# A two-layer encoder trunk on one core: first weights in halves, turns block by block, Silu behind the last norm, and the last norm's second column half prepared ahead

## The chip, the core and the metric

The kernel runs on one core of one Trainium2 chip. The metric is the device time of one execution in microseconds. TensorE is PE in the profile (its weight loads are PEld), VectorE is DVE, ScalarE is ACT, GpSimd is POOL, SyncE is SP; SPq, ACTq and POOLq are the queues from which these engines issue DMAs.

## The reference: what is computed

Two requests, 512 and 256 tokens of 1024 features, go through the same two layers. Each layer is a macaron block, and a final RMSNorm closes the trunk:

```python
x = x + 0.5 * swiglu_ffn(rmsnorm(x, g0), w1a, w2a)    # D 1024, DFF 2816
x = x + mixer(rmsnorm(x, g1))                          # layer 0: HGRN2, layer 1: windowed attention
x = x + 0.5 * swiglu_ffn(rmsnorm(x, g2), w1b, w2b)

def swiglu_ffn(x, w1, w2):
    gate, up = split(x @ w1)
    return (silu(gate) * up) @ w2
```

All is float32. The first operation is thus RMSNorm of the input and the first half of a feed-forward (called f0 in the kernel), the last is a feed-forward's second product, the residual add, and RMSNorm with the gain `g_final`.

## The kernel before

The 768 tokens are six blocks of 128 rows, three to a half (`H` = 384 tokens). A float32 product is made of three products in the format f32r: a tile is split into a high part (a CAST on ACT) and a low part (a subtraction on DVE), and `mm3` (L368 to L370) adds high by high, high by low and low by high. Most of the feed-forwards' products go by a scheme of seven block products in place of eight (p1 to p7, which need sums of blocks); the first two of the 22 column pieces of f0's first weight are made plainly, by `up_plain`.

**Pools.** Raw weights are loaded to four buffers `wr`, their split parts lie in eight buffers `w`. PSUM has eight banks; a bank is given to a new tile when the last reader of the old one is done.

**The order of the work** is that in which the program issues it, engine by engine, but a step can be tied behind another one with `issue_after`, and the scheduler moves it to where that allows. Each engine then works its list in order and waits at an instruction whose inputs are missing.

**The beginning.** `setup` (L103 to L125) loads an identity matrix, casts it to `ident_r`, and transposes the norms' gains on PE to get them as columns (`cols`, COPY at L125). `load_x` (from L378) issues the loads of blocks 0 to 2, of the first two weights of 512 KB each (L168, `load_next`), then of blocks 3 to 5, on SP's queue; later loads follow. `norm_block` (L411) makes a Square with a running sum on ACT (L418; for block 1 a DVE instruction, L416), a Sqrt (L419), a RECIPROCAL (L420) and a TENSOR_SCALAR (L421) that gives the normed block. `turn` (L425) transposes: for each of the eight column pieces, three transposes (L439), one per block, fill one PSUM bank, then ACT multiplies by the gain's column and writes the high part (L446), and DVE writes the low part (L447). `stage_next` splits a weight by `plain_steps` (L191 CAST, L192 subtraction). The second half's blocks come as deferred steps (`rest` and two more turns, with evictions at L450, and sums at L408, L509 and L523 for the seven-product scheme). Between them PE begins with f0's plain products: four weights, each against the eight pieces of a half of the tokens; these are what the text calls the first, second, third and fourth weight (gate and up for piece 0, then gate and up for piece 1). A gate's product goes through Silu on ACT (L608, `gated`), and DVE multiplies by the up product (L610). Sqrt and Silu need different tables of ACT, so a change between them shows as an ACT_TABLE_LOAD.

**The end.** In the last `down_last`, the blocks of the second half of the tokens (3 to 5) get their last residual add on DVE (L811), and behind each stands `final_block` (L1500): Square with sum over 1024 columns (L1504), Sqrt (L1505), RECIPROCAL (L1506), one DVE instruction that multiplies by the reciprocal and by `g_final` (L1511), and the output's DMA on SP's queue (L1512); for the last block the latter two go in two column halves.

Of the kernel before, what the change touches and what calls it, by code (L numbers as in the profile page):

```python
# [16 lines left out]
P = 128  # L17
# [17 lines left out]
H = T // 2  # L35
HB = H // P
PLAIN = {"f0": 2, "f1": 1, "f2": 1, "f3": 1}
GATED = 2
# [19 lines left out]
class Trunk:  # L58
# [44 lines left out]
    def setup(self, consts):  # L103
        nc, cp = self.nc, self.cp
        self.consts = consts
        ident, rows = consts[0], consts[4]
        self.eps = cp.tile([P, 1], F32, name="eps")
        nc.vector.memset(self.eps, EPS)
        warm = self.stat(1)
        nc.scalar.activation(warm, self.eps, AF.Sqrt)  # L110
        raw = self.tmp(P)
        nc.scalar.dma_start(raw, ident)
        self.identr = cp.tile([P, P], F32R, name="ident_r")
        nc.vector.tensor_copy(self.identr, raw)
# [42 lines left out]
    def load_next(self):  # L157
# [5 lines left out]
        for src in srcs:  # L163
            t = self.wp.tile([P, 1024], F32, tag="wr", name=self.name("wr"), bufs=RAWBUFS)
            raw = t[:, : shape[0] * shape[1]].rearrange("p (a b) -> p a b", a=shape[0])
            if len(srcs) < 4:
                src = src.rearrange("(k p) c -> p k c", p=P)
            self.last_load = self.nc.sync.dma_start(raw, src)  # L168
            raws.append(raw)
# [17 lines left out]
    def plain_steps(self, key, raw, shape):  # L187
        def go():
            n = shape[0] * shape[1]
            hi, lo = (self.wtile()[:, :n].rearrange("p (a b) -> p a b", a=shape[0]) for _ in range(2))  # L190
            self.nc.scalar.copy(hi, raw)  # L191
            self.nc.vector.tensor_sub(lo, raw, hi.bitcast(F32))  # L192
            self.staged[key] = (hi, lo, 2)

        return [(2, go, False)]

# [179 lines left out]
    def load_x(self, srcs):  # L376
# [14 lines left out]
        for b in range(HB):  # L391
            with self.tc.issue_after(order) if order else nullcontext():
                order = self.norm_block(b, vector=b == 1) or order
        self.turn(0, 0, 0, True)
        self.turn(0, 1, 0, True)
        with self.tc.issue_after(order):
            self.stage_next()
            self.stage_next()
        self.load_tables()

        def rest():
            for b in range(HB, NBLK):
                self.norm_block(b)
            for part in range(2):
# [19 lines left out]

    def turn(self, half, part, row, first=False):  # L425
        nc = self.nc
# [8 lines left out]
        for m in range(4 * part, 4 * part + 4):  # L435
# [4 lines left out]
            g = self.cols[:, row * NC + m : row * NC + m + 1]  # L440
            if first:
                name, kp = f"b{part}{half}", m % 4 // 2
                if (name, kp) not in self.ops:
                    self.ops[(name, kp)] = self.big([P, 2, 2, H], F32R)
                hi, lo = self.operand(name, m % 4)
                nc.scalar.activation(hi, pt, AF.Copy, scale=g)  # L446
                nc.vector.scalar_tensor_tensor(lo, pt, g, hi.bitcast(F32), ALU.mult, ALU.subtract)  # L447
                continue
            if feeds_ffn:
# [4 lines left out]
            nc.vector.scalar_tensor_tensor(lo, pt, g, hi.bitcast(F32), ALU.mult, ALU.subtract)  # L454
        if feeds_ffn and not first:
            for kp in range(2):
                self.put(f"b{part}{half}", kp, self.tn[(part, half)][:, kp])
# [305 lines left out]
    def down_last(self, tag, hid, tail, next_row):  # L763
# [5 lines left out]
        for name in LAST:  # L769
# [4 lines left out]
            for i in range(HB):  # L774
# [725 lines left out]
    def final_block(self, b):  # L1500
        nc = self.nc
        outs = self.out_args[1]
        y, r = self.big([P, D]), self.stat(1)
        nc.scalar.activation(y, self.x[b], AF.Square, accum_out=r)  # L1504
        nc.scalar.activation(r, r, AF.Sqrt, bias=self.eps, scale=1.0 / D)  # L1505
        nc.vector.reciprocal(r, r)  # L1506
        s, row = (0, b * P) if b * P < TA else (1, b * P - TA)
        width = 512 if b == NBLK - 1 else D
        for lo in range(0, D, width):
            sl = slice(lo, lo + width)  # L1510
            nc.vector.scalar_tensor_tensor(y[:, sl], self.x[b][:, sl], r, self.g_final[:, sl], ALU.mult, ALU.mult)  # L1511
            nc.sync.dma_start(outs[s][row : row + P, sl], y[:, sl])  # L1512

    def load_final(self):
        self.g_final = self.big([P, D])
        with self.tc.issue_after(self.last_load.ins):
# [249 lines left out]
```

## Time and profile before

| | us |
|---|---|
| median of three runs | 2752.88 (2752.06, 2752.88, 2753.34) |
| the profiled execution | 2753.83 |
| its span, first to last instruction | 2752.0 |
| PE busy | 2730.4 |
| DVE busy | 2191.9 |
| ACT busy | 1409.2 |
| PE's first matmul | 7.41 |
| PE's first weight product | 14.39 |
| last output DMAs issued from | 2748.18 |

The three runs lie within 1.3 us. The profiled execution has 1.83 us outside its span. Times inside the span count from its start. The page gives busy time by engine; the timeline gives start, duration and engine of neighbouring instructions of one group, the idle time before them in brackets and what ended it; the windows view gives busy time of each engine in a stretch.

### The profile page before, as it was taken

How to read it: one execution, taken by the hardware profiler on the slowest of the kernel's cores; microseconds unless marked ns; L12 is line 12 of the kernel's file. 1: busy time of each engine (PE TensorE's matmuls, PEld its weight loads, DVE VectorE, ACT ScalarE, POOL GpSimd, SP SyncE). 2: the span in 40 equal slices, each digit the busy share in tenths (PEclk: the TensorE clock that was granted, in tenths of full speed). 3: DMA queues.
4: the chain of work that ended last, by engine and by line, in shares of the span. 5: the costliest groups of instructions: out<-in, count | busy, mean ns of one | idle time of the engine just before them, and what ended most of it. 6: DMA issues, size and time to landing. Idle time of an engine off the chain costs nothing.

```text
span 2752.0 us, 41062 instructions
## 1 busy us (share of the span) xinstructions
PE 2730.4 (99%) x15045; PEld 2538.4 (92%) x15045; DVE 2191.9 (80%) x3784; ACT 1409.2 (51%) x2654; POOL 477.1 (17%) x537
## 2 busy tenths in 40 slices
PE   8999999999999999999999999999999999999998
PEld 8999999989999889999998999999888889999997
DVE  8788788767877789788878987887847869788877
ACT  7444444634454776444455643444458855444443
POOL 1111121200000111211121121112005621211120
PEclk9999999999999999999999999999999999999999
DMA  6554556751123655655455565546424435555453
GB/s 170 134 127 111 127 140 165 220 152 32 47 55 70 193 136 127 146 134 125 118 135 138 117 146 129 130 114 141 129 78 111 89 75 121 143 134 131 119 130 112
DMA packets 362970, 340.70 MB, mean 124 GB/s; under 512 B 15288, under 2 KB 275344, under 8 KB 362768
## 3 DMA queue, kind: packets, MB, share of 16 engines
q1 hardware_dynamic: 306912, 227.18, 28.0%
q0 software_dynamic: 51552, 97.41, 20.4%
q10 hardware_dynamic: 4304, 13.49, 1.4%
q8 instruction: 118, 1.93, 0.3%
q14 instruction: 84, 0.69, 0.1%
HBM read 228.45 MB, written 15.73 MB: 89 GB/s over the span
## 4 chain that ended last, share of the span: by engine, by line
PE 80%; DVE 1%; ACT 1%; DMA 1%; issue 0%; SPq 0%; DVEq 0%; POOL 0%; ACTq 0%; POOLq 0%
PE ps L641 33%; PE ps L750 13%; PE ps L964 6%; PE ps L783 5%; PE ps L368 5%; PE ps L369 5%; PE ps L370 5%; PE ps L1027 3%; PE ps L1132 1%; PE ps L439 1%; PE ps L1620 1%; PE ps L1108 1%; PE ps L1632 0%; PE ps L1582 0%; PE ps L1633 0%; PE ps L1583 0%
## 5 line engine op out<-in xcount | busy, mean ns | idle before, releaser
L641 PE MATMUL ps<-big,w 128*128 128x384 f32 x6972 | 1213.3, 334 | 0.0
L641 PEld LDWEIGHTS ps<-big,w 128*128 128x128 f32 x6972 | 1209.4, 188 | 1.5
L228 ACT CAST w<-wr 128x512 fp32r<-128x512 f32 (+1 forms) x615 | 429.7, 706 | 664.1 <-PE ps L641 339.9
L229 DVE TENSOR_TENSOR w<-wr,w 128x512 fp32r<-128x512 f32 (+1 forms) x538 | 435.7, 813 | 142.9 <-ACT w L228 118.0
L750 PE MATMUL ps<-w,big 128*128 128x512 f32 x2016 | 461.2, 390 | 0.0
L750 PEld LDWEIGHTS ps<-w,big 128*128 128x128 f32 x2016 | 376.7, 188 | 80.4 <-ACT big L373 1.7
L155 POOL DMA_DIRECT2D s<-wr x135 | 118.8, 891 | 1209.2 <-DVE wr L235 357.0
L811 DVE SCALAR_TENSOR_TENSOR x<-ps,x 128x512 f32<-128x512 f32 x420 | 272.8, 681 | 13.0 <-PE ps L783 12.6
L374 DVE TENSOR_TENSOR big<-tA,big 128x384 fp32r<-128x384 f32 x308 | 189.5, 626 | 22.1 <-ACT big L373 21.7
L155 POOL DMA_DIRECT2D wr<-wr x115 | 101.4, 882 | 527.3 <-DVE big L374 166.7
L373 ACT CAST big<-tA 128x384 fp32r<-128x384 f32 x308 | 152.7, 514 | 74.7 <-DVE tA L675 29.6
L368 PE MATMUL ps<-big,w 128*128 128x384 f32 x544 | 187.4, 345 | 1.5 <-DVE big L447 0.8
L369 PE MATMUL ps<-big,w 128*128 128x384 f32 x544 | 182.9, 336 | 0.1
L370 PE MATMUL ps<-big,w 128*128 128x384 f32 x544 | 182.7, 336 | 0.0
L964 PE MATMUL ps<-w,big 128*128 128x512 f32 x756 | 178.2, 393 | 0.1
L783 PE MATMUL ps<-w,big 128*128 128x512 f32 x756 | 174.7, 391 | 1.3 <-DVE x L811 1.3
L783 PEld LDWEIGHTS ps<-w,big 128*128 128x128 f32 x756 | 141.1, 188 | 31.4 <-DVE x L811 2.5
L964 PEld LDWEIGHTS ps<-w,big 128*128 128x128 f32 x756 | 140.3, 188 | 29.0 <-DVE w L374 0.6
L229 POOL TENSOR_TENSOR w<-wr,w 128x512 fp32r<-128x512 f32 x77 | 112.9, 1466 | 104.7 <-ACT w L228 99.6
L669 DVE TENSOR_TENSOR tA<-tA,ps 128x384 f32<-128x384 f32 x80 | 44.0, 550 | 83.5 <-PE ps L641 83.5
L235 DVE TENSOR_TENSOR wr<-wr,wr 128x512 f32<-128x512 f32 (+1 forms) x120 | 110.0, 916 | 0.2 <-DVE w L229 0.2
L368 PEld LDWEIGHTS ps<-big,w 128*128 128x128 f32 x544 | 102.3, 188 | 2.2 <-ACT w L191 1.1
(237 smaller groups left out, 3700.9 us busy)
## 6 DMA issues: line engine op xcount, KB each, us to landing
wr<-in_ffn_w_dram SPq DMA_DIRECT2D x256, 512.0 KB, 4.0
s<-wr POOLq DMA_DIRECT2D x135, 256.0 KB, 4.7
s<-in_ffn_w_dram SPq DMA_DIRECT2D x126, 256.0 KB, 3.2
wr<-wr POOLq DMA_DIRECT2D x86, 256.0 KB, 4.2
wr<-in_hg_w_in_dram SPq DMA_DIRECT2D x32, 512.0 KB, 3.9
wr<-wr POOLq DMA_DIRECT2D x29, 512.0 KB, 4.6
spill<-x ACTq DMA_DIRECT2D x12, 512.0 KB, 4.3
kept<-big POOLq DMA_DIRECT2D x8, 768.0 KB, 6.2
```

What stands on the lines that cost most here:

```text
L155: self.nc.gpsimd.dma_start(out, src, accum_op=ALU.add)
L228: nc.scalar.copy(h, src)
L229: (eng or nc.vector).tensor_sub(l, src, h.bitcast(F32))
L368: nc.tensor.matmul(out, a[0], b[0], start=first, stop=False)
L369: nc.tensor.matmul(out, a[0], b[1], start=False, stop=False)
L370: nc.tensor.matmul(out, a[1], b[0], start=False, stop=last)
L374: self.last_lo = self.nc.vector.tensor_sub(lo, src, hi.bitcast(F32)).ins
L641: self.nc.tensor.matmul(ps, a[x], b[y], start=first and k == 0 and i == 0, stop=k == 3 and i == 2, skip_group_check=True,)
L750: nc.tensor.matmul(ps, a[x], w[y], start=name == chain and kp == 0 and q == 0, stop=kp == 1 and q == 2, skip_group_check=True,)
L783: nc.tensor.matmul(ps, a[x], w[y], start=name == chain and k == 0 and q == 0, stop=k == 2 and q == 2, skip_group_check=True,)
L811: self.nc.vector.scalar_tensor_tensor(x, ps, c, x, ALU.mult, ALU.add)
L964: nc.tensor.matmul(ps, x[:, sl], y, start=fresh and k == 0 and q == 0, stop=k == 3 and q == 2, skip_group_check=True,)
```

## The change

At the **beginning**, five things.

1. The first two weights of f0 (`EARLY`) are loaded in two halves of 128x4x128 each, and split half by half: four loads, four casts and four subtractions in place of two of each.
2. The turns of the first half go block by block (`first_turns`): eight PSUM banks are taken at once, block 0's eight transposes come first, then block 1's, then block 2's; the evictions follow in the order of the pieces. The first weight's second half is split behind the fourth piece, the second weight behind the last.
3. Twenty products of the identity with itself, 128x128 in f32r, are put on PE ahead of the transpose that makes `cols`. Nothing reads their result.
4. The first Silu is tied behind the Sqrt of block 5's norm (`self.last_norm`, passed to `gated`).
5. By the scheduler, other instructions move with it: on DVE the COPY of `cols` stands behind block 1's normed tile rather than ahead of block 0's, and the third and fourth weights' casts stand elsewhere on ACT (below).

At the **end**, for blocks 3 to 5, `final_part` squares the second column half with its sum (that half's residual add is done earlier, at p5), turns the sum into a bias, and multiplies that half by `g_final` ahead of time. `final_block` then squares the first half alone, takes the Sqrt with that bias, multiplies the first half on DVE as before, and the second half by the reciprocal on ACT. The two halves are issued as DMAs of their own, the last block's second half on ACT's queue.

```diff
+EARLY = (("f0", 0, 0), ("f0", 0, 1))
...
+        idle = self.ps(P)
+        for _ in range(20):
+            nc.tensor.matmul(idle, self.identr, self.identr, start=True, stop=True)
...
-            self.last_load = self.nc.sync.dma_start(raw, src)
+            step = shape[0] // 2 if key in EARLY else shape[0]
+            for lo in range(0, shape[0], step):
+                self.last_load = self.nc.sync.dma_start(raw[:, lo : lo + step], src[:, lo : lo + step])
...
-        self.turn(0, 0, 0, True)
-        self.turn(0, 1, 0, True)
         with self.tc.issue_after(order):
             self.stage_next()
-            self.stage_next()
+        self.first_turns()
+        for _ in range(2):
+            with self.tc.issue_after(self.last_hi):
+                self.stage_next()
...
             for b in range(HB, NBLK):
-                self.norm_block(b)
+                self.last_norm = self.norm_block(b)
...
+    def first_turns(self):
+        nc = self.nc
+        self.h, self.ops, self.tn = None, {}, {}
+        pts = [self.ps(H) for _ in range(NC)]
+        for i in range(HB):
+            for m, pt in enumerate(pts):
+                nc.tensor.transpose(pt[:, i * P : (i + 1) * P], self.xn[i][:, m * P : (m + 1) * P], self.ident)
+        for m, pt in enumerate(pts):
+            g = self.cols[:, m : m + 1]
...
+            hi, lo = self.operand(name, m % 4)
+            with self.tc.issue_after(self.last_hi):
+                last = nc.scalar.activation(hi, pt, AF.Copy, scale=g).ins
+            nc.vector.scalar_tensor_tensor(lo, pt, g, hi.bitcast(F32), ALU.mult, ALU.subtract)
+            self.last_hi = last
+            if m == 3:
+                with self.tc.issue_after(self.last_hi):
+                    self.stage_next()
...
-                    t = ts[2 * j + half] = self.gated(pss)
+                    t = ts[2 * j + half] = self.gated(pss, None if j or half else self.last_norm)
...
+                elif name == "p5" and next_row is None:
+                    self.final_part(HB + i)
...
+        y, bias = self.final[b]
+        r = self.stat(1)
+        lo, hi = halves
+        nc.scalar.activation(y[:, lo], self.x[b][:, lo], AF.Square, accum_out=r)
+        nc.scalar.activation(r, r, AF.Sqrt, bias=bias, scale=1.0 / D)
+        nc.vector.reciprocal(r, r)
+        nc.vector.scalar_tensor_tensor(y[:, lo], self.x[b][:, lo], r, self.g_final[:, lo], ALU.mult, ALU.mult)
+        nc.sync.dma_start(out[:, lo], y[:, lo])
+        nc.scalar.activation(y[:, hi], y[:, hi], AF.Copy, scale=r)
+        (nc.scalar if b == NBLK - 1 else nc.sync).dma_start(out[:, hi], y[:, hi])
+
+    def final_part(self, b):
+        nc = self.nc
         y, r = self.big([P, D]), self.stat(1)
+        hi = slice(512, D)
+        nc.scalar.activation(y[:, hi], self.x[b][:, hi], AF.Square, accum_out=r)
+        nc.scalar.activation(r, r, AF.Identity, bias=self.eps, scale=1.0 / D)
+        nc.vector.tensor_mul(y[:, hi], self.x[b][:, hi], self.g_final[:, hi])
+        self.final[b] = y, r
```

On every engine the order of the instructions differs only in about the first hundred and the last fifteen rows; between them it is the same. Line numbers of the changed kernel differ: split CAST and subtraction are L382 and L383 there, Square L428, Sqrt L429, `mm3` L377 to L379, later turns L470 with their evictions L473, Silu L631, multiplication L633.

ACT at the beginning, before: block 5's Square (`x_108`), the first Silu with a table load on either side, the casts of the third and fourth weight (`w_310`, `w_374`) and the first evictions of the second half's turns.

```order
L418 ACTIVATE big_250,stat_251<-x_108 128x1024
L608 ACT_TABLE_LOAD
L608 ACTIVATE tA_304<-ps_203 128x384
L419 ACT_TABLE_LOAD
L419 ACTIVATE stat_251<-stat_251,eps 128x1
L191 CAST w_310<-wr_184 128x1024
L191 CAST w_374<-wr_186 128x1024
L450 ACTIVATE big_278<-ps_274,cols 128x384
L450 ACTIVATE big_278<-ps_280,cols 128x384
```

The same place now: block 5's Square (`x_131`), the third weight's cast (`w_337`), the Sqrt, one table load, Silu, and the first eviction.

```order
L428 ACTIVATE big_277,stat_278<-x_131 128x1024
L382 CAST w_337<-wr_155 128x1024
L429 ACTIVATE stat_278<-stat_278,eps 128x1
L631 ACT_TABLE_LOAD
L631 ACTIVATE tA_331<-ps_230 128x384
L473 ACTIVATE big_305<-ps_301,cols 128x384
```

The fourth weight's cast isn't there. It stands 16 rows behind the Silu, after all eight evictions of the second half's turns and seven casts of their sums (`w_401`, the tenth row here):

```order
L382 CAST big_334<-tA_331 128x384
L473 ACTIVATE big_358<-ps_354,cols 128x384
L473 ACTIVATE big_358<-ps_360,cols 128x384
L473 ACTIVATE big_358<-ps_365,cols 128x384
L473 ACTIVATE big_358<-ps_370,cols 128x384
L382 CAST big_375<-big_358 128x2x384
L382 CAST big_378<-big_358 128x2x384
L382 CAST big_394<-big_286 128x2x384
L382 CAST big_398<-big_286 128x2x384
L382 CAST w_401<-wr_157 128x1024
L631 ACTIVATE tA_462<-ps_341 128x384
```

So Sqrt and Silu each stand once, the third weight's cast went ahead of the Sqrt, and the fourth weight's cast went from right behind the third's to behind 15 other instructions.

PE at the same place, before: the last products of the third weight, then the first ones of the fourth.

```order
L368 MATMUL ps_314<-big_171,w_310 128x384
L369 MATMUL ps_314<-big_171,w_310 128x384
L370 MATMUL ps_314<-big_171,w_311 128x384
L368 MATMUL ps_386<-big_132,w_374 128x384
L369 MATMUL ps_386<-big_132,w_374 128x384
L370 MATMUL ps_386<-big_132,w_375 128x384
```

And now, where `w_151` is the first weight, used again for the other half of the tokens:

```order
L379 MATMUL ps_341<-big_208,w_338 128x384
L377 MATMUL ps_413<-big_191,w_401 128x384
L378 MATMUL ps_413<-big_191,w_401 128x384
L377 MATMUL ps_468<-big_322,w_151 128x384
L378 MATMUL ps_468<-big_322,w_151 128x384
L379 MATMUL ps_468<-big_322,w_152 128x384
```

The first two products with the fourth weight stand where they stood, directly behind the third's; ten products with the first weight were put between them and the products that need the fourth weight's low part.

More of the change, by code (lines that the diff above doesn't have):

```diff
@@ L187, in plain_steps, with go @@
     def plain_steps(self, key, raw, shape):
-        def go():
+        step = shape[0] // 2 if key in EARLY else shape[0]
+        def go(at):
             n = shape[0] * shape[1]
[L190 to L195, printed above, removed]
+            if at == 0:
+                hi, lo = (self.wtile()[:, :n].rearrange("p (a b) -> p a b", a=shape[0]) for _ in range(2))
+                self.staged[key] = (hi, lo, 2)
+            hi, lo = (t[:, at : at + step] for t in self.staged[key][:2])
+            self.split(raw[:, at : at + step], hi, lo)
+        return [(0 if at else 2, lambda at=at: go(at), False) for at in range(0, shape[0], step)]
     def quad_steps(self, key, raws, srcs, order):
@@ L423, in norm_block, with turn @@
         return last
-    def turn(self, half, part, row, first=False):
+    def first_turns(self):
[7 more added lines that the diff above has]
+            g = self.cols[:, m : m + 1]
+            name, kp = f"b{m // 4}0", m % 4 // 2
+            if (name, kp) not in self.ops:
+                self.ops[(name, kp)] = self.big([P, 2, 2, H], F32R)
+            hi, lo = self.operand(name, m % 4)
[6 more added lines that the diff above has]
+                    self.stage_next()
+    def turn(self, half, part, row):
         nc = self.nc
@@ L440, in turn @@
             g = self.cols[:, row * NC + m : row * NC + m + 1]
[L441 to L448, printed above, removed]
             if feeds_ffn:
@@ L454, in turn @@
             nc.vector.scalar_tensor_tensor(lo, pt, g, hi.bitcast(F32), ALU.mult, ALU.subtract)
-        if feeds_ffn and not first:
+        if feeds_ffn:
             for kp in range(2):
@@ L1502, in final_block @@
         outs = self.out_args[1]
-        y, r = self.big([P, D]), self.stat(1)
[L1504 to L1512, printed above, removed]
+        s, row = (0, b * P) if b * P < TA else (1, b * P - TA)
+        out = outs[s][row : row + P, :]
+        halves = [slice(lo, lo + 512) for lo in (0, 512)]
+        if b < HB:
+            y, r = self.big([P, D]), self.stat(1)
+            nc.scalar.activation(y, self.x[b], AF.Square, accum_out=r)
+            nc.scalar.activation(r, r, AF.Sqrt, bias=self.eps, scale=1.0 / D)
+            nc.vector.reciprocal(r, r)
+            nc.vector.scalar_tensor_tensor(y, self.x[b], r, self.g_final, ALU.mult, ALU.mult)
+            nc.sync.dma_start(out, y)
+            return
+        y, bias = self.final[b]
[3 more added lines that the diff above has]
+        nc.scalar.activation(r, r, AF.Sqrt, bias=bias, scale=1.0 / D)
+        nc.vector.reciprocal(r, r)
+        nc.vector.scalar_tensor_tensor(y[:, lo], self.x[b][:, lo], r, self.g_final[:, lo], ALU.mult, ALU.mult)
[4 more added lines that the diff above has]
+        nc = self.nc
+        y, r = self.big([P, D]), self.stat(1)
+        hi = slice(512, D)
[3 more added lines that the diff above has]
+        self.final[b] = y, r
     def load_final(self):
+        self.final = {}
         self.g_final = self.big([P, D])
```

## The prediction

> **What bounds the kernel now.** I read the page's engine line first, then the windows view of the stretch behind the beginning, then the two wait lists, then the timelines of the first 40 us and of the last 8.
>
> ```profile
> PE 2730.4 (99%) x15045; PEld 2538.4 (92%) x15045; DVE 2191.9 (80%) x3784; ACT 1409.2 (51%) x2654; POOL 477.1 (17%) x537
> 31.30:70.70 39.40, 39.40 (x229) 39.30 (x227) 39.40 (x60) 25.09 (x42) 6.10 (x6) 1.00 0.44 111
> PE ps L368 <- DVE big L447: 0.8, 1, 0.8
> PE ps L368 <- ACT w L191: 0.7, 1, 0.7
> DVE w L192 <- ACT w L191: 1.9, 1, 1.9
> DVE stat L420 <- ACT stat L419: 0.4, 1, 0.4
> ```
>
> The first row says that PE is busy for 2730.4 of 2752.0 us; what any edit can win is the 21.6 us at the two ends. The second (busy us of PE, PEld, DVE, ACT, POOL between 31.30 and 70.70) says that from 31.3 us on PE has no hole, and DVE none either. The last four are all waits that PE has between 14 and 75 us and that DVE has between 12 and 71, counted from 0.1 us up: one each for the first product, the third weight, the first subtraction and one RECIPROCAL. So the rule for this case is: a shift of PE at 31 us is carried to the last block, us for us, and nothing behind it gives it back. Only the path to that point, and the tail, have to be walked.
>
> PE, ACT and DVE in that stretch (start, time of the row's instructions together, engine, line; an xN row holds N of them):
>
> ```profile
> 8.99 4.63 PE L439 MATMUL ps<-ident_r,big 128*128 128x128 f32 x24 [1.20 <-DVE big L421]
> 14.39 0.45 PE L368 MATMUL ps<-big,w 128*128 128x384 f32 x1 [0.77 <-DVE big L447]
> 25.16 0.45 PE L368 MATMUL ps<-big,w 128*128 128x384 f32 x1 [0.75 <-ACT w L191]
> 26.96 0.44 PE L370 MATMUL ps<-big,w 128*128 128x384 f32 x1
> 28.80 0.49 PE L439 MATMUL ps<-ident_r,big 128*128 128x128 f32 x3
> 31.23 0.33 PE L368 MATMUL ps<-big,w 128*128 128x384 f32 x1
> ```
> ```profile
> 11.51 1.05 ACT L191 CAST w<-wr 128x1024 fp32r<-128x1024 f32 x1 [2.45 <-DMA wr<-in_ffn_w_dram]
> 12.46 3.88 ACT L446 ACTIVATE big<-ps,cols 128x384 fp32r<-128x384 f32 x8
> 16.18 1.09 ACT L191 CAST w<-wr 128x1024 fp32r<-128x1024 f32 x1
> 17.12 1.11 ACT L418 ACTIVATE big<-x 128x1024 f32<-128x1024 f32 x1
> 20.77 1.28 ACT L608 ACT_TABLE_LOAD   x1
> 22.58 1.28 ACT L419 ACT_TABLE_LOAD   x1
> 24.08 1.98 ACT L191 CAST w<-wr 128x1024 fp32r<-128x1024 f32 x2
> 26.36 2.00 ACT L450 ACTIVATE big<-ps,cols 128x384 f32<-128x384 f32 x4 [0.30 <-PE ps L439]
> 35.07 1.28 ACT L608 ACT_TABLE_LOAD   x1
> ```
> ```profile
> 19.57 0.16 DVE L420 RECIPROCAL stat<-stat 128x1 f32<-128x1 f32 x1 [0.42 <-ACT stat L419]
> 22.76 1.82 DVE L408 TENSOR_TENSOR big<-big 128x768 f32<-128x768 f32 x2
> 24.57 0.54 DVE L610 TENSOR_TENSOR tA<-tA,ps 128x384 f32<-128x384 f32 x1
> 25.02 0.75 DVE L421 TENSOR_SCALAR big<-x,stat 128x1024 f32<-128x1024 f32 x1
> 25.68 1.22 DVE L192 TENSOR_TENSOR w<-wr,w 128x1024 fp32r<-128x1024 f32 x1
> ```
>
> The chain to see: first weight lands 11.5, ACT rounds it and evicts the eight turns (12.46 to 16.2), two Squares and a Sqrt follow, DVE's RECIPROCAL of block 3 at 19.57 releases a run of 12 DVE instructions without a hole that ends with the third weight's low part, and PE takes that at 26.96. The fourth weight's CAST is the second of the pair at 24.08 and is done by 26.1, five microseconds before PE wants it at 31.23: nobody waits for it now.
>
> **The beginning: first weights in halves, turns block by block.** The landing moves first. The row below is the DMA rate in 40 slices of 1 us; the other two are a pair of half-size casts from later in the program.
>
> ```profile
> GB/s 0 4 198 404 407 413 276 97 123 276 294 310 373 406 426 364 323 291 290 289 285 296 290 292 187 22 102 158 156 127 237 341 291 177 92 170 129 133 0 0
> 4.94 1.01 SPq L168 DMA_DIRECT2D wr<-in_ffn_w_dram  x2
> 52.06 1.14 ACT L228 CAST w<-wr 128x512 fp32r<-128x512 f32 x2 [1.45 <-PE ps L369]
> ```
>
> Half a weight is 256 KB, which at the 276 to 310 GB/s of slices 9 to 11 takes 0.9 us; so the first half lands about 0.9 earlier. From one cast's start to what follows on ACT a whole weight takes 0.95 (11.51 to 12.46); of the 1.14 for two halves I give the first 0.52 and the last 0.62, since a last row shows its full latency, as the 1.05 does. The first eviction goes from 12.46 to 12.46 - 0.9 - 0.43, about 11.1. Two more issues stand on SP's queue ahead of blocks 3 to 5, at 0.5 each; the DMA rate stays above 270 GB/s from slice 9 on, so the transfers are limited by bytes, not by issues, and I cost them at nothing; if that cover fails, block 5 and the third weight land up to 1.0 later, which is about what either has in hand before ACT takes it (Square of block 5 at about 18.9 by the walk, the cast at about 20).
>
> By the turns PE must keep up. Two windows of the transposes, and an f32r transpose from the middle of the program:
>
> ```profile
> 9.90 0.75 DVE L421 TENSOR_SCALAR big<-x,stat 128x1024 f32<-128x1024 f32 x1
> 9.00:12.60 3.60, 3.60 (x17) 3.45 (x18) 1.00 1.02 309
> 12.70:13.60 0.90, 0.90 (x8) 0.68 (x6) 1.00 1.02 405
> 2009.90:2010.90 1.00, 0.80 (x8) 0.65 (x7) 1.00 0.00 0
> 4.95 0.23 DVE L114 CAST ident_r<-tB 128x128 fp32r<-128x128 f32 x1 [4.08 <-DMA tB<-in_ident_dram]
> ```
>
> Busy PE, 17 transposes took 3.60 us (0.21 each) up to 12.6 and 8 took 0.90 (0.11 each) behind it, so PE ran at half speed for its first 3.7 us of steady work (8.99 to 12.7) and at full speed from there. The 20 identity products begin at 5.2, when ident_r is cast, and last between 20 x 0.11 and 20 x 0.21, to 7.4 or 9.4; they run in PE's idle time, delay at most the turn of block 0, and should bring the doubling to about 9. Then block 2's normed tile (9.90 + 0.75 now; 0.4 earlier without the `cols` copy ahead) is transposed at once and the first eviction hangs on the weight: 11.1. If the products don't bring the doubling, 16 transposes of 0.21 stand ahead of block 2's, and the first eviction comes at about 12.3. The Trainium skill, "TensorE: Matmul & The Clock Gate", section "Part 4: PE-mode transpose", says that transposes don't engage the full clock; the trace disagrees as far as it can, since only transposes ran from 9.0 to 12.7 and their spacing halved; by that page the late case of 12.3 would hold.
>
> From the first eviction to the RECIPROCAL of block 3 was 19.57 - 12.46 = 7.11, with one cast of 0.95 in it, the second weight's. Now three half casts stand there, the first weight's second half (between the evictions) and the second weight's two: 7.11 - 0.95 + 3 x 0.52 = 7.72. RECIPROCAL: 11.1 + 7.72 = 18.8, 0.75 earlier. The run of 12 DVE instructions behind it is the same in another order, so the third weight's low part reaches PE at 26.96 - 0.75 = 26.2.
>
> **Silu behind the last norm.** It removes the table loads at 22.58 and 35.07, 2.6 us of ACT. Neither was on the path: DVE's run had no hole between 19.57 and 31.3. Worth nothing by itself. What it moves is worth more: by ACT's order the fourth weight's CAST no longer stands beside the third's but behind eight evictions and seven casts, which wait for block 5's norm.
>
> **The fourth weight.** PE finishes the third weight's products 31.23 - 26.96 = 4.27 after their low part, less three transposes (0.33) that now go ahead of them: 26.2 + 3.9 = 30.1. Ready by then, the weight would give PE a gain of 1.1. But ACT: block 5's TENSOR_SCALAR ended at 25.77, 6.20 behind the RECIPROCAL; an L408 (0.87) and the L610 (0.45) now go behind it, so it ends 4.88 behind, at 23.7, and the evictions start 0.3 later, at 24.0 (they no longer wait for casts, as at 26.06). The same 15 instructions took from 26.36 to 35.07 = 8.7 without a hole; DVE, which feeds three of them, is ahead by its 0.75. The CAST starts at 32.7. From the CAST pair's start to PE was 25.16 - 24.08 = 1.08. PE gets the fourth weight at 33.8 instead of 31.23: **+2.55**, a stall of 3.7 us, in which its in-order queue holds back ten products with the first weight that would have been ready. The low part follows within the 12 products that come ahead of its use (12 x 0.17 = 2.1), so it adds nothing. Bounds: first eviction 10.6 to 11.5, 0.3 either way in the evictions' start: +1.8 to +3.3.
>
> **The end.** The timelines of the last block, with its issues:
>
> ```profile
> 2744.93 0.69 DVE L811 SCALAR_TENSOR_TENSOR x<-ps,x 128x512 f32<-128x512 f32 x1
> 2745.65 1.06 ACT L1504 ACTIVATE big<-x 128x1024 f32<-128x1024 f32 x1 [0.56 <-DVE x L811]
> 2746.84 0.29 ACT L1505 ACTIVATE stat<-stat,eps 128x1 f32<-128x1 f32 x1
> 2747.36 1.41 DVE L1511 SCALAR_TENSOR_TENSOR big<-x,stat,big 128x512 f32<-128x512 f32 x2
> 2748.18 0.96 SPq L1512 DMA_DIRECT2D out_dram<-big  x2
> out_dram<-big SPq DMA_DIRECT2D x2, 256.0 KB, 2.2
> ```
>
> Half a Square saves 0.45, but block 4's copy of its second half now stands on ACT ahead of the last Sqrt and takes back about 0.4. RECIPROCAL stays near 2747.2. The gain is that the two output halves are made beside each other, on DVE and ACT, and issued on two queues: the last issue at 2748.15 instead of 2748.7. Both carry the same bytes behind block 4's, so I take **-0.4**, between 0 (bytes limit) and -0.7 (issue limits). The second-half Squares and products at p5 are off the path: ACT is half idle, and PE has the rest of the block's products to run.
>
> **The sum.** +2.55 - 0.4 = +2.15. The profiled execution took 2753.83 (span 2752.0 and 1.83 around it), 0.95 above the median of the three runs; it goes to 2756.0, the median 2752.88 to **2755.0**. A difference of 0.2%, 5.5 us, is about what a measurement of this kernel can tell from none; the forecast is within it. Its own range, +1.8 - 0.7 to +3.3, is 2754.0 to 2756.2.
>
> **Rivals.**
> *The weight is there in time.* ACT's order speaks against it, which has the CAST behind 15 others; it would need the CAST by 29.0, 3.7 us before the walk has it. Then -1.1 - 0.4 = -1.5: 2751.4. Chance 0.08.
> *The clock falls in the new hole.* No row of before shows PE idle for over 0.8 us behind 14.39, so nothing shows that full speed outlives 3.7 us of nothing; full speed took 3.7 us of work to come. If it falls, the next 3.7 us go at half speed, which loses half of that, 1.85: +4.0, 2756.9. If it stays low for two such stretches, because the idle straddles two and the return starts late, 3.7 are lost: +5.85, **2758.7**, slower by over 0.2%. It decides once the hole exceeds what the clock tolerates, somewhere above 0.8 us. The Trainium skill, same page, "Why this matters for your kernels", asks for no PE idle gap over about 3 us, which would halve the clock: it speaks against this change, and no run here shows it yet. Chances 0.20 and 0.04.
> *The early full clock does not come.* First eviction 12.3, all behind it 1.2 later: +3.35, 2756.2. For it: nothing shows that the identity products count as work. Against it: transposes did. Chance 0.12.
>
> **Numbers.** Forecast 0.54, the four cases above 0.44, anything else 0.02. The range takes in the forecast, one half-speed stretch and the late start with their bounds, and one us below the forecast's own low end for a CAST that ACT reaches sooner than walked; it stops short of the weight in time and of two stretches: 2753.0 to 2757.4. Faster by over 0.2% (under 2747.4) is reached by no case: 0.01. Slower by over 0.2% (above 2758.4) by two stretches or one on top of a late start: 0.05. Within: 0.94.
>
> **What would show it.** In the profile after: one PE wait on ACT's cast of over 3 us near 30 to 34 us, the CAST behind a second group of evictions, first eviction near 11.1, third weight's low part near 26; matmuls at 0.17 spacing right behind the stall (0.35 would be the clock); PE without holes from there; last issue near 2748.15 plus the shift. The forecast is wrong if that wait is below 1 us, if PE has a second hole behind it, or if the tail's gain exceeds 1 us.

## The result, and the profile after

The changed kernel takes 2761.21 us (median of 7 runs, 2760.59 to 2762.95), the kernel before 2752.49 (7 runs, 2751.4 to 2753.5): a ratio of 1.0033, 95% interval 1.0021 to 1.0044. It is **slower, by 8.7 us**; I had forecast +2.1 and a range that ends at 2757.4. The profiled execution of the changed kernel took 2760.59, its span is 2758.8.

From the lists of PE's and of DVE's waits of the changed kernel in the first 75 us (us in all, times, longest):

```profile
PE ps L377 <- ACT w L382: 3.5, 1, 3.5
```
```profile
DVE big L450 <- ACT big L449: 1.8, 1, 1.8
```

The 3.5 us on ACT's cast of a weight is the wait that the prediction named, and PE's longest there behind the first instruction. The second row is one that it did not name: DVE waits 1.8 for the first eviction, which was to come early.

PE's timeline of the beginning (start, time of the row's instructions together), then ACT's and DVE's:

```profile
5.22 4.53 PE L119 MATMUL ps<-ident_r 128*128 128x128 f32 x20 [5.22 <-DVE ident_r L115]
9.55 0.37 PE L127 MATMUL ps<-ident_r,tB 88*128 88x88 f32 x1
9.71 3.84 PE L441 MATMUL ps<-ident_r,big 128*128 128x128 f32 x24
...
27.95 0.44 PE L379 MATMUL ps<-big,w 128*128 128x384 f32 x1 [0.43 <-DVE w L383]
...
35.53 0.51 PE L377 MATMUL ps<-big,w 128*128 128x384 f32 x1 [3.47 <-ACT w L382]
35.83 0.52 PE L378 MATMUL ps<-big,w 128*128 128x384 f32 x1
```
```profile
9.53 0.62 ACT L382 CAST w<-wr 128x512 fp32r<-128x512 f32 x1 [0.45 <-DMA wr<-in_ffn_w_dram]
12.83 2.00 ACT L449 ACTIVATE big<-ps,cols 128x384 fp32r<-128x384 f32 x4 [2.68 <-PE ps L441]
...
25.85 2.00 ACT L473 ACTIVATE big<-ps,cols 128x384 f32<-128x384 f32 x4 [1.16 <-PE ps L470]
...
34.38 1.09 ACT L382 CAST w<-wr 128x1024 fp32r<-128x1024 f32 x1
```
```profile
20.56 0.16 DVE L430 RECIPROCAL stat<-stat 128x1 f32<-128x1 f32 x1 [1.02 <-ACT stat L429]
```

The half weight is there early (cast at 9.53), and ACT then stands idle for 2.68 us until PE has filled the first bank: the identity products held PE to 9.55, at 0.21 each, and the transposes came behind them. The first eviction is 0.37 later than before (12.83 against 12.46), the RECIPROCAL 0.99. Further on the fourth weight reaches PE at 35.53 against 31.23, 4.30 later, and from there the products are 0.32 apart instead of 0.17.

The windows view says what that is (busy us of PE, PEld, DVE, ACT and POOL, then the granted clock, the DMA share and GB/s):

```profile
32.35:35.76 3.41, 0.23 (x1) 0.24 (x2) 3.41 (x5) 3.41 (x5) 0.85 (x1) 1.00 0.44 77
35.76:39.17 3.41, 3.41 (x12) 3.41 (x12) 3.41 (x5) 1.03 (x3) 0.00 (x0) 0.50 0.13 33
39.17:42.58 3.41, 3.41 (x22) 3.41 (x21) 3.41 (x5) 2.23 (x3) 0.65 (x1) 1.00 0.42 125
```

A stretch of 3.41 us with PE busy for 0.23 is followed by one of the same length at a granted clock of 0.50. The 12 products behind the wait take 3.75 (the next one, in the timeline, starts at 39.28) in place of 12 x 0.173 = 2.08: 1.67 lost. 4.30 + 1.67 = 5.97, and it is carried: in DVE's timeline the first residual add (L811, now L836), at 84.45 before, is at 90.33, 5.88 later.

```profile
84.45 0.68 DVE L811 SCALAR_TENSOR_TENSOR x<-ps,x 128x512 f32<-128x512 f32 x1
90.33 0.68 DVE L836 SCALAR_TENSOR_TENSOR x<-ps,x 128x512 f32<-128x512 f32 x1
```

The tail, in the timeline of all engines:

```profile
2751.41 0.69 DVE L836 SCALAR_TENSOR_TENSOR x<-ps,x 128x512 f32<-128x512 f32 x1 [0.49 <-PE ps L806]
...
2752.77 0.71 ACT L1547 ACTIVATE big<-big,stat 128x512 f32<-128x512 f32 x1
...
2753.38 0.28 ACT L1543 ACTIVATE stat<-stat,stat 128x1 f32<-128x1 f32 x1
...
2753.89 0.72 ACT L1547 ACTIVATE big<-big,stat 128x512 f32<-128x512 f32 x1 [0.23 <-DVE stat L1544]
2753.89 0.75 DVE L1545 SCALAR_TENSOR_TENSOR big<-x,stat,big 128x512 f32<-128x512 f32 x1
2754.64 0.37 ACTq L1548 DMA_DIRECT2D out_dram<-big  x1
2754.67 0.33 SPq L1546 DMA_DIRECT2D out_dram<-big  x1
```

From the last residual add to the end of the span it takes 2758.8 - 2751.41 = 7.4 us, before 2752.0 - 2744.93 = 7.1. The issues stand 3.26 behind the add, where the last one was some 3.9 behind it, as forecast; but the span's end is now 4.1 behind the last issue instead of 3.2. That both halves' bytes leave behind that one issue is the likely reason; no run separates it.

### The profile page after: what moved, and what is told of

Its sections match the earlier page's. It is cut to its first block, busy times and chain, and to the rows that moved or that the text cites. A ratio compares the mean times of both kernels' runs of the same rounds, so it can differ in the third digit from the quotient of the medians.

```text
span 2758.8 us, 41125 instructions
## 1 busy us (share of the span) xinstructions
PE 2735.8 (99%) x15065; PEld 2543.2 (92%) x15065; DVE 2194.1 (80%) x3788; ACT 1408.8 (51%) x2666; POOL 477.9 (17%) x537
## 4 chain that ended last, share of the span: by engine, by line
PE 96%; ACT 2%; DVE 1%; DMA 0%; issue 0%; POOL 0%; SPq 0%; ACTq 0%; DVEq 0%; POOLq 0%
PE ps L664 43%; PE ps L773 17%; PE ps L806 6%; PE ps L989 6%; PE ps L377 5%; PE ps L378 5%; PE ps L379 5%; PE ps L1052 3%; PE ps L1157 1%; PE ps L470 1%; PE ps L1666 1%; PE ps L1133 1%; PE ps L1678 0%; PE ps L1628 0%; PE ps L1679 0%; PE ps L1629 0%
## 5 line engine op out<-in xcount | busy, mean ns | idle before, releaser
L664 PEld LDWEIGHTS ps<-big,w 128*128 128x128 f32 x6972 | 1209.4, 188 | 1.4 <-ACT tA L724 0.2
L836 DVE SCALAR_TENSOR_TENSOR x<-ps,x 128x512 f32<-128x512 f32 x420 | 273.1, 683 | 11.5 <-PE ps L806 11.1
L383 DVE TENSOR_TENSOR big<-tA,big 128x384 fp32r<-128x384 f32 x308 | 190.9, 631 | 20.7 <-ACT big L382 20.5
L377 PE MATMUL ps<-big,w 128*128 128x384 f32 x544 | 188.0, 346 | 4.0 <-ACT w L382 3.5
L382 ACT CAST big<-tA 128x384 fp32r<-128x384 f32 x308 | 152.7, 514 | 76.8 <-DVE tA L698 30.9
L379 PE MATMUL ps<-big,w 128*128 128x384 f32 x544 | 183.2, 337 | 0.4 <-DVE w L383 0.4
L383 DVE TENSOR_TENSOR w<-wr,w 128x1024 fp32r<-128x1024 f32 (+1 forms) x74 | 88.0, 1194 | 30.6 <-ACT w L382 29.8
L382 ACT CAST w<-wr 128x1024 fp32r<-128x1024 f32 (+1 forms) x74 | 75.8, 1030 | 70.2 <-PE ps L378 35.9
```

The source lines that it names most:

```text
L377: nc.tensor.matmul(out, a[0], b[0], start=first, stop=False)
L379: nc.tensor.matmul(out, a[1], b[0], start=False, stop=last)
L382: self.last_hi = self.nc.scalar.copy(hi, src).ins
L383: self.last_lo = self.nc.vector.tensor_sub(lo, src, hi.bitcast(F32)).ins
L664: self.nc.tensor.matmul(ps, a[x], b[y], start=first and k == 0 and i == 0, stop=k == 3 and i == 2, skip_group_check=True,)
L836: self.nc.vector.scalar_tensor_tensor(x, ps, c, x, ALU.mult, ALU.add)
```

## The experiments

Medians in us; "before" is the kernel before on the same chip. With the Silu tied, ACT's order has the fourth weight's cast behind eight evictions and seven casts; with the Silu free it has it beside the third's.

| kernel | median | before | difference | 95% interval of the ratio |
|---|---|---|---|---|
| changed, once more | 2761.01 | 2752.62 | +8.4 | 1.0019 to 1.0044 |
| changed, Silu free | 2756.59 | 2752.62 | +4.0 | 1.0005 to 1.0023 |
| before, Silu tied | 2758.24 | 2752.62 | +5.6 | 1.0012 to 1.0031 |
| changed, hole filled | 2758.31 | 2752.62 | +5.7 | 1.0013 to 1.0030 |
| before, new end | 2752.72 | 2752.45 | +0.3 | 0.9993 to 1.0010 |
| before, identity products | 2754.97 | 2752.45 | +2.5 | 1.0001 to 1.0019 |
| changed, no identity products | 2759.90 | 2752.45 | +7.4 | 1.0017 to 1.0038 |
| changed, fourth weight with the third | 2756.28 | 2752.45 | +3.8 | 1.0004 to 1.0022 |
| before, halves | 2751.80 | 2752.42 | -0.6 | 0.9990 to 1.0007 |
| before, halves, block by block | 2754.93 | 2752.42 | +2.5 | 1.0000 to 1.0018 |
| changed, Silu free, wide products | 2755.39 | 2752.42 | +3.0 | 1.0001 to 1.0018 |
| the same, two sums on POOL | 2756.68 | 2752.42 | +4.3 | 1.0007 to 1.0025 |

**The tie, taken out and put in alone.**

```diff
 # changed, Silu free
-                    t = ts[2 * j + half] = self.gated(pss, None if j or half else self.last_norm)
+                    t = ts[2 * j + half] = self.gated(pss)
 # before, Silu tied
-                self.norm_block(b)
+                self.last_norm = self.norm_block(b)
-                    t = ts[2 * j + half] = self.gated(pss)
+                    t = ts[2 * j + half] = self.gated(pss, None if j or half else self.last_norm)
```

Silu free: 

> The changed kernel with the Silu free again (gated without last_norm); all else as changed. In this order of ACT the fourth weight's cast is back beside the third's, ahead of the evictions. Theory A (the tie moved that cast, and the wait for it with the half clock behind it is most of the loss): no PE wait on a cast over 1 us, no half-speed stretch near 36 us, only the late RECIPROCAL (+1.0) and the tail (+0.3) stay: about 2753.8, 2753 to 2755. Theory B (the loss comes from the identity products, the halves or the tail): still 2758 or more.

Silu tied in the kernel before: 

> The kernel before with one edit: the first Silu behind block 5's Sqrt. By the order the fourth weight's cast goes behind eight evictions and seven casts, as in the changed kernel. Theory A: a PE wait of 3 to 4 us on that cast near 31 to 34.5 us, shift of +3.3 there, and +1.6 more where the clock falls for one window of 3.4 us: 2755.8 without, 2757.4 with the half clock. Theory B: two table loads fewer, nothing else: 2752.5.

The tie alone costs 5.6 us, taking it out gives 4.4 back. That is Theory A, but only half of what was expected of the free Silu came: 2756.6 and not 2753.8. Its profile shows where. The beginning costs about what was expected: the first residual add is at 85.58, 1.1 later than in the profile before, though with a wait of 1.6 on the third weight's cast that was not expected. Another 1.25 are lost between that add and the last one (0.6 of it in a wait that the next section takes up), and 0.3 in the tail; and the execution of the profile before is itself 1.3 above the median from which 2753.8 was reckoned. The tied kernel has the same wait of PE on the cast, 3.5 us, and two stretches at half speed behind it in the windows view:

```profile
30.38:33.79 3.41, 0.70 (x5) 0.38 (x3) 3.41 (x5) 3.41 (x6) 0.28 (x1) 1.00 0.44 132
33.79:37.20 3.41, 2.64 (x8) 2.57 (x9) 3.41 (x5) 1.11 (x2) 0.58 (x1) 0.50 0.44 77
37.20:40.62 3.42, 3.42 (x12) 3.42 (x12) 3.42 (x5) 3.13 (x4) 0.00 (x0) 0.50 0.52 153
```

Here the hole spans two stretches: 0.70 us of work in the first brings the clock down, 2.64 of 3.41 in the second is not enough to bring it back, a full third one does. This is the second of the two forms that the prediction gave this rival: 6.06 us of products at half speed (34.56 to 40.62) lose 3.0, and the time is 0.8 above the 2757.4 that was expected with one such stretch.

**The fourth weight staged with the third.**

```diff
             wh, wl = self.take((tag, j, c))
+            if tag == "f0" and j == 1 and half == 0 and c == 0:
+                with self.tc.issue_after(self.last_hi):
+                    self.take((tag, 1, 1))
```

> The changed kernel with the fourth weight staged together with the third; by the order its cast then stands behind four evictions and three casts in place of eight and seven. Theory A: cast at about 29.6, done before PE wants it at 31.9, no wait over 0.5 us and no half clock: start +0.7, tail +0.3: about 2753.5, with the tie still in. Theory B (the tie itself or other edits cost the time): 2758 or more.

The timeline of ACT has the cast 4.4 us earlier than in the changed kernel:

```profile
29.98 1.07 ACT L382 CAST w<-wr 128x1024 fp32r<-128x1024 f32 x1
```

PE has no wait on a cast and no stretch at half speed up to 75 us. The tie stays in, the time is that of the free Silu (2756.28): the tie costs by the place of this one cast, not by the Silu. Like that of the free Silu, the time is 2.8 above what was expected.

**The hole filled.**

```diff
             ps = self.ps(H)
+            if tag == "f0" and j == 1 and half == 0 and c == 1:
+                for _ in range(22):
+                    nc.tensor.matmul(ps, self.identr, self.operand("b00", 0)[0], start=True, stop=True)
```

> The changed kernel with 22 products of 384 columns more, which nothing reads, written to the bank of the fourth weight's product; by the order 6 stand ahead of the third weight's low products and 16 behind them, and 4 products with the first weight then go ahead of the fourth weight's. The cast stays as late as it is. Theory A with the clock (a hole of PE over 3.4 us halves the clock for a window): hole filled, no half-speed stretch, 4 products done early: 1.6 + 0.7 = 2.3 less than the changed kernel, 2758.9. If the half speed had another cause than the hole, it stays: 2760.5.

PE's timeline, where the 16 products stand in the hole:

```profile
33.11 2.94 PE L620 MATMUL ps<-big,ident_r 128*128 128x384 f32 x16
35.89 0.35 PE L377 MATMUL ps<-big,w 128*128 128x384 f32 x1
36.08 0.34 PE L378 MATMUL ps<-big,w 128*128 128x384 f32 x1
```

The cast is as late as ever, the products behind it are 0.17 apart, and the time falls by 2.7: the half speed came from the hole.

**The changed kernel once more.** 

> The changed kernel once more, for a second profile. 2761.2; Theory A: the same wait of 3.5 us on the fourth weight's cast. If the clock is set by windows that run free of the program, full speed comes at another moment than 11.85, and the half-speed stretch behind the wait begins at another moment than 35.76, or doesn't come; if it is set by the work itself, both come at the same moments again.

The half speed came again, at another moment: 37.62 to 41.04, behind 0.98 us of work in 3.41. And full speed came later. The windows view, the first ahead of it and the second up to it:

```profile
6.90:10.31 3.41, 3.41 (x18) 3.41 (x18) 2.54 (x7) 2.14 (x5) 0.54 (x1) 1.00 0.91 255
10.31:13.73 3.42, 3.42 (x18) 3.42 (x17) 1.59 (x4) 0.00 (x0) 0.00 (x0) 1.00 1.05 371
```

In both PE is busy throughout, with instructions 0.21 apart (the view's clock column tells of lowerings behind the first rise only). The first stretch holds identity products and a few transposes and brings nothing; the second holds transposes, and at its end, 13.73, their spacing falls to 0.11. The first eviction was at 13.86, one us later than in the first profile, and this execution took 2761.77 against 2760.59. The program began 0.3 later and full speed came 1.9 later: so the stretches of 3.41 us run free of the program, and where they fall moves the start: of the 1.0 by which the first eviction is later, the later beginning makes only 0.3.

**Identity products alone, and all but them.** The three lines put into the kernel before, or taken out of the changed one.

Alone: 

> The kernel before with the twenty identity products alone. Theory A (they run at half speed from 5.2 to 9.5, hold up the transpose for the gains' columns, and full speed comes little earlier): first eviction 0.3 to 0.7 later than 12.46, 2752.8 to 2753.2. As predicted, full speed by 9 us: no later start, 2752.5 or a little less.

All but them: 

> The changed kernel without the identity products; the late cast of the fourth weight stays in its order. Theory A: columns ready by 8.1 again, first eviction near 12.1 to 12.4 in place of 12.83, everything behind it earlier by the same, the wait of 3.5 us and the half clock stay: 0.4 to 0.7 less than the changed kernel, about 2760.6. Theory B (the identity products cause the loss): near 2754.

Alone they cost 2.5 us, where Theory A had 0.3 to 0.7; without them the changed kernel takes 1.1 less (2761.01 against 2759.90), though the two intervals overlap. They won nothing in either; how much of the cost is their own is less clear. PE's timeline of the former reads as above (20 in 4.53, transposes from 9.67), and ACT idles ahead of its first eviction with a whole weight rounded:

```profile
9.83 1.05 ACT L194 CAST w<-wr 128x1024 fp32r<-128x1024 f32 x1 [0.80 <-DMA wr<-in_ffn_w_dram]
13.33 3.88 ACT L449 ACTIVATE big<-ps,cols 128x384 fp32r<-128x384 f32 x8 [2.45 <-PE ps L442]
```

The first eviction stands 3.66 behind the first transpose. In the profile of the new end (below), which has the beginning of the kernel before, it is 11.90 - 9.24 = 2.66, with the transposes 0.21 apart in both. So about five more transposes stand ahead of the first full bank: the three lines also moved the order of the transposes, which the edit was not meant to do, and this accounts for 1.0 of the 1.4 by which the first eviction is later.

In the other pair the profiles show no gain at the start. PE's transposes and ACT's first eviction of the changed kernel without the identity products:

```profile
9.22 4.34 PE L438 MATMUL ps<-ident_r,big 128*128 128x128 f32 x24 [1.20 <-DVE big L428]
12.84 2.00 ACT L446 ACTIVATE big<-ps,cols 128x384 fp32r<-128x384 f32 x4 [2.41 <-PE ps L438]
```

The transposes begin 0.5 earlier, but full speed came at 12.35 in this execution and at 11.87 in the other, and the first eviction is at 12.84 against 12.83, the first residual add at 90.43 against 90.33. The 1.1 by which these two executions differ is lost behind that, where the changed kernel's profile has a wait that this one lacks (taken up at the end of the next section).

**Halves, then halves with the turns block by block.** The loads and splits in halves put into the kernel before, with the old turns; then with `first_turns`.

Halves: 

> The kernel before with the first two weights in halves alone (four loads, casts and subtractions); turns in the old order, no identity products, Silu free, old end. By the order the first eviction stands behind three half casts, the third of them of the second weight. Theory A (halves cost ACT and DVE a little and win nothing, since the first eviction waits for transposes at half speed): first eviction 12.0 to 12.6, RECIPROCAL 18.9 to 19.3, against 19.0 in a before-like start whose weight lands in time: 0 to +0.3 us, 2752.5 to 2752.8. As predicted for the halves (first eviction 1 us earlier): 2751.6.

Block by block as well: 

> The same with the turns block by block as well; no identity products, Silu free, old end. Theory A: in the old order the first eviction needs 11 transposes, block by block 17, six more at 0.21 while PE is at half speed: first eviction 12.8, RECIPROCAL 20.5, about +1.5: 2754.0. If the order of the transposes costs nothing: as halves alone, 2752.5 to 2752.8.

Halves alone are 0.6 below the kernel before, the best of all kernels tried, though its interval holds 1; block by block on top costs 3.1. ACT's first eviction of the two:

```profile
11.19 0.62 ACT L379 CAST w<-wr 128x512 fp32r<-128x512 f32 x1 [0.28 <-DMA wr<-in_ffn_w_dram]
11.79 3.88 ACT L452 ACTIVATE big<-ps,cols 128x384 fp32r<-128x384 f32 x8
```
```profile
13.29 1.99 ACT L446 ACTIVATE big<-ps,cols 128x384 fp32r<-128x384 f32 x4 [3.04 <-PE ps L438]
```

At 11.79 ACT goes from its casts into the evictions without a hole, at 13.29 it has waited 3.04 us for PE. In the old turns' order the first bank was full after 11 transposes (from 9.13), in the new one after 17 (from 9.36), all of them 0.21 apart. The block-by-block profile also has a hole that the prediction had not thought of, ahead of the third weight, and it lowers the clock too:

```profile
23.70:27.12 3.42, 1.55 (x10) 0.96 (x9) 3.42 (x6) 3.39 (x5) 2.15 (x2) 1.00 0.59 135
27.12:30.53 3.41, 3.41 (x17) 3.41 (x16) 3.41 (x5) 2.61 (x6) 0.18 (x1) 0.50 0.97 178
```

**The end alone.** `final_part` and the new `final_block` put into the kernel before. 

> The kernel before with the end part of the change alone (second column half squared and multiplied ahead, two output halves beside each other, the last one on ACT's queue). Theory A (both halves' bytes leave together behind one issue latency, so the last landing is no earlier): 0 to +0.3 us, 2752.5 to 2752.8. As predicted: -0.4. If the end part carries the 2 us by which the medians differ more than the two profiles: +2.

 It measured +0.3, which its interval does not tell from nothing. No gain came from it.

Its profile is worth a look for another reason, since its beginning is that of the kernel before:

```profile
10.68 1.05 ACT L191 CAST w<-wr 128x1024 fp32r<-128x1024 f32 x1 [1.68 <-DMA wr<-in_ffn_w_dram]
11.90 3.89 ACT L446 ACTIVATE big<-ps,cols 128x384 fp32r<-128x384 f32 x8 [0.17 <-PE ps L439]
```

The first weight landed 0.8 earlier than in the profile from which I predicted. In the profile with the Silu tied, whose beginning is the same, it landed as late as there (cast at 11.54), so this moment varies from run to run. The execution from which I predicted took 2753.83, more than any of the seven runs (2751.4 to 2753.5).

PE's transposes of this profile begin here:

```profile
9.24 4.98 PE L439 MATMUL ps<-ident_r,big 128*128 128x128 f32 x24 [1.20 <-DVE big L421]
```

**Full speed by other products, and less work for DVE.** 17 products of 384 columns over a tile of ones in place of the identity products, Silu free; then two sums on POOL.

```diff
+        plain = self.tmp(H)
+        nc.vector.memset(plain, 1.0)
+        wide = self.tmp(H, F32R)
+        nc.vector.tensor_copy(wide, plain)
+        idle = self.ps(H)
+        for _ in range(17):
+            nc.tensor.matmul(idle, wide[:, :P], wide, start=True, stop=True)
...
 # the second kernel also
-                    nc.vector.tensor_add(self.tn[(part, 0)][:, kp], o[:, :, 0, :], o[:, :, 1, :])
+                    (nc.gpsimd if part else nc.vector).tensor_add(self.tn[(part, 0)][:, kp], o[:, :, 0, :], o[:, :, 1, :])
```

> The changed kernel with the Silu free and with 17 products of 384 columns over a tile of ones from about 2 us in place of the twenty identity products; nothing reads them. Theory C (full speed comes behind windows that wide products fill): full speed by 9 us, transposes 0.11 each, first eviction 10.5 to 10.9, no hole: 2752 to 2754.3, and 2.4 us less than the same kernel with identity products (2756.6). Rival (products ahead of the transposes bring no earlier full speed, as the identity products brought none): full speed between 11.9 and 13.7, first eviction 12.4 or later: 2756.

> The former with two of the four sums of high and low parts moved from DVE to POOL. Theory: DVE's run behind the RECIPROCAL ends 1.7 earlier, and so does the third weight's low part: 2750.5 to 2752.6, below both kernels. Rival: POOL takes over 2 us for each sum and DVE waits for them, or DVE is the bound until 70 us in any case: not below the former.

The windows view and ACT's timeline of the first:

```profile
3.38:6.79 3.41, 3.41 (x13) 3.41 (x12) 1.12 (x2) 1.45 (x3) 0.00 (x0) 1.00 1.01 381
8.90:11.50 2.60, 2.60 (x24) 2.60 (x24) 1.98 (x5) 1.05 (x3) 0.67 (x1) 1.00 1.12 286
```
```profile
10.45 0.62 ACT L386 CAST w<-wr 128x512 fp32r<-128x512 f32 x1 [1.62 <-DMA wr<-in_ffn_w_dram]
11.01 1.52 ACT L453 ACTIVATE big<-ps,cols 128x384 fp32r<-128x384 f32 x3
```

Theory C's mechanism holds: wide products fill a stretch, all 24 transposes then take 0.11 each, and the first eviction hangs on the weight, at 11.01, as the prediction had wanted of the identity products. The time did not follow: the median is 2755.39, above the 2754.3 at which the expectation ended. In the profiled execution, 2753.7, the first residual add is at 83.54, 0.9 earlier than in the profile before, but 1.5 is lost in the wait in the middle that is taken up below. The eleven runs reach from 2752.0 to 2756.9. This kernel still has the hole ahead of the third weight, a wait of 1.6; that the clock falls there in some of its runs would explain a part of the spread. The granted clock on record for each run fits this (0.998 in the five that took 2755.8 or more, 0.999 or 1.000 in the other six), but no profile of such a run shows it. With two sums on POOL it is no faster: DVE's two subtractions beside them took 3.77 us in place of 1.28.

## Why the prediction was wrong

*The fourth weight* was right as a mechanism. The walk had the evictions start 5.2 behind the RECIPROCAL, 8.7 from there to the cast, 1.08 from cast to product; measured were 5.29, 8.53 and 1.15. The wait was 3.5 where I had 3.7. The Trainium skill's caution on PE's idle gaps ("TensorE: Matmul & The Clock Gate", "Why this matters for your kernels"), which no run showed when I cited it, is borne out by the four profiles here that have the hole of 3.5 us. Its figure of about 3 us is no safe limit here: in the profile with halves and turns block by block a wait of 1.6 was enough.

*The start failed.* "The first eviction hangs on the weight: 11.1" came out as 12.83 and 13.86. Two steps of it were wrong. I let the identity products bring full speed to about 9, because transposes had brought it; they brought none, and at half speed they kept PE from the transposes until 9.71. And I priced "block by block" at nothing where full speed comes early: it puts six more transposes ahead of the first full bank, 6 x 0.21 = 1.3 at half speed, and cost 3.1 in all on top of the halves. That step alone was enough to lose the 11.1, since without the identity products the first eviction is at 12.84. The price of the late case, 12.3, was too low as well: it let the transposes begin at 8.99, ahead of the end of the identity products. The halves did what I said and won nothing in this kernel, since PE was later than the weight. All that hangs on the RECIPROCAL came 1.8 later than walked, the fourth weight with it: 35.53 where I had 33.8.

*The half clock in the hole* I had at +1.85 and chance 0.20; it was +1.67 in the profile after, about 1.7 in two of the other three with the 3.5 us wait, and 3.0 with the Silu tied alone, the case that I gave 0.04. The windows show why it was likelier than that: wherever the stretches of 3.41 fall, a hole of 3.5 leaves one of them with at most (2 x 3.41 - 3.5) / 2 = 1.66 us of work, and 1.55 was seen to bring the clock down. That makes it likely and not certain, since 1.53 of other work did not (last section).

*The rivals were not exclusive.* I gave the late start and the half clock 0.12 and 0.20 as two ways to miss, and the range took in each by itself. Both rest on one question, how fast PE's clock comes and goes, and both came true. By my own prices that would have been 2.15 + 1.2 + 1.85 = +5.2, 2758.1.

*The end* was -0.4 and came as nothing or a little more than nothing: of its two bounds it is the 0 of "bytes limit" that held.

*The sum.* Between the two profiles I had forecast +2.15. To this came 1.75 by the late start, 1.67 by the clock, 0.7 at the end (+0.3 for -0.4) and 0.6 in the middle, 6.9 together; the spans differ by 6.8.

*The two profiles* lie nearer to each other than the medians, which differ by 8.7. In the profile from which I walked the first weight landed late (cast at 11.51), which hid a first eviction that could come at 11.9; its execution is 1.3 above its kernel's median. The execution profiled after is 0.6 below its own, and the lowest of its seven.

What stays open is a us or so in the middle. The changed kernel's profile has a wait that the profile before lacks, at 1098 us, in the list of waits of PE behind 75 us:

```profile
PE ps L773 <- DVE x L836: 1.2, 1, 1.2
```

It is there, with 0.6 to 1.5, in seven profiles: the two of the changed kernel, the identity products alone, the Silu free, the fourth weight with the third, and the two with wide products. It is missing in the kernel before, the Silu tied alone, the two with halves, the new end, the filled hole and the changed kernel without identity products. So every profile that has it is of a kernel with idle products at the beginning, and of those kernels only the one with the filled hole lacks it; part of what these products cost may lie here. In the profiles that have it, ACT waited 4.5 to 5.4 us there for an accumulating DMA, in the others for 3.6 at most. Why that transfer lands later was not tried.

## What to carry to other kernels

A tie that saves table loads on an idle engine can move another instruction on that engine behind a long run; read the whole order of that engine, and ask who waits for what was moved. Rivals that rest on one unknown (here: PE's clock) are to be added up as well as taken singly. Work that is to raise PE's clock must be shown to raise it, and a hole of PE is to be priced with what follows it at half speed.

## What the runs showed of the hardware

- The granted clock changed only at steps of 3.41 us (in the changed kernel's profile at 11.87, 35.76, seven steps on, and 39.17), whose phase differs from run to run (rises at 11.87 and 13.73 of the same kernel). Behind the beginning, stretches with PE busy for 0.23, 0.65, 0.70, 0.98 and 1.55 us were followed by half speed; one with 1.88 was not; 2.64 did not restore full speed, 3.41 did. The windows that aren't shown above, of the changed kernel without identity products:

```profile
32.83:36.24 3.41, 0.65 (x4) 0.65 (x5) 3.41 (x5) 3.10 (x5) 0.86 (x1) 1.00 0.45 77
```

  of the changed kernel once more:

```profile
34.21:37.62 3.41, 0.98 (x5) 0.98 (x6) 3.41 (x5) 2.77 (x4) 0.10 (x1) 1.00 0.45 79
```

  and of the changed kernel with the Silu free, followed by full speed:

```profile
22.63:26.04 3.41, 1.88 (x13) 1.33 (x11) 3.41 (x6) 3.37 (x5) 1.34 (x2) 1.00 0.71 190
```

  Busy time alone does not decide. In the profile before, the last stretch with work, 1.53 us of 512-column products, was still followed by full speed; of the 1.55 above 0.66 were transposes, the rest 384-column products. So the border is not one number of busy time.

```profile
2743.36:2746.77 3.41, 1.53 (x7) 0.94 (x5) 3.34 (x6) 2.56 (x5) 0.00 (x0) 1.00 0.28 114
2746.77:2750.19 3.42, 0.00 (x0) 0.00 (x0) 1.82 (x4) 0.33 (x2) 0.00 (x0) 1.00 0.77 307
```

- A stretch filled with 128-column f32r identity products, but for a few transposes at its end (6.90 to 10.31 above), did not raise the clock; one of transposes did, and one of 384-column products did. Why the first don't count was not settled.
- POOL's two sums of 128x768 f32 slowed DVE's subtractions beside them: two of 128x512 took 3.77 us, 1.28 without. The timeline of DVE:

```profile
16.49 3.77 DVE L387 TENSOR_TENSOR w<-wr,w 128x512 fp32r<-128x512 f32 x2
```
